# One ring of small feed-forward buffers split into two: thirteen slots for evicted products, three for weight differences

## The chip, the cores and the metric

The kernel runs on one core of one Trainium2 chip. The metric is the device time of one execution in microseconds (us). The engines are TensorE (PE; its weight loads are listed apart as PEld), VectorE (DVE), ScalarE (ACT), GpSimd (POOL) and SyncE (SP), which here issues the transfers.

## The reference

One decoder layer in float32 for 1024 tokens of width 1024: a feed-forward with half weight, a token mixer (dilated window attention beside a gated DeltaNet, merged by gates), a second feed-forward, and a final norm. The change touches the two feed-forwards alone.

```python
def swiglu(x, w_gate, w_up, w_down):
    return (jax.nn.silu(x @ w_gate) * (x @ w_up)) @ w_down

# D_MODEL = 1024, SEQ = 1024, D_FF = 2816
x = x + 0.5 * swiglu(rmsnorm(x, ffn1_norm), ffn1_w_gate, ffn1_w_up, ffn1_w_down)
h = rmsnorm(x, mix_norm)
x = x + hybrid_mixer(h, ...)
x = x + 0.5 * swiglu(rmsnorm(x, ffn2_norm), ffn2_w_gate, ffn2_w_up, ffn2_w_down)
return rmsnorm(x, final_norm)
```

## The kernel before

Every float32 product is made of three products of halves: each operand is split into a high part (a cast, fH for weights) and the remainder (a subtraction, fL), and high x high, low x high and high x low are summed in PSUM. Weights are split by `ff_split`: ACT casts (L207), DVE subtracts (L208). Both results live in rings of nine tiles, fH and fL.

**The hidden part** (`ff_hidden`, once for each feed-forward, at about 46 to 464 us and 2079 to 2515 us) computes silu(x Wg) * (x Wu), one block of 128 hidden columns after another, 22 blocks in all. The first two blocks are done plainly. The other twenty go in ten pairs through `ff_pair` and `ff_products`: a pair of blocks, two halves of the width and two halves of the tokens make a 2x2 matrix product, done with seven products of blocks instead of eight, as in Strassen's scheme. The price is sums and differences of blocks: of the tokens once, of the weights for every pair. The first pair has the order FIRST, the nine others the order STEPS: products 1, 6, 5, 7, 2, 4, 3, each first for the gate matrix (i = 0), then for the up matrix (i = 1). One product of one matrix is 12 matmuls (four pieces of the width by three halves) on 512 tokens, so a pair is 168 matmuls on line L366. They accumulate in four PSUM banks named mm, tC, tM and tA (two tiles each, one for gate and one for up); product 1 is in mm, products 6, 7 and 4 in tC, and product 2 is in mm again.

The weights of a pair come in two transfers of 1 MB (L216, `fraw`, a ring of two: gate and up). `prepare(n, i)` makes the left operand of product n for matrix i out of the four quarters a11, a12, a21, a22 of such a tile. For product 6 DVE makes three differences or sums: s3 = a11 - a21 into a small tile (L323), a21 += a22 (L324), a11 = a21 - a11 (L325); then a11 is split. s3 is the operand of product 7, a21 that of product 5.

After each product the bank is evicted into small tiles of 128 x 512 which `ff_e` gives out: p1 by ACT (L370), u2 (L373) and u3 (L378, L379) by DVE, then silu on ACT (L381, L388, L395, L402) and the product of gate and up on DVE (L383, L390, L397, L404). L378 evicts product 7 and reads bank tC, on which product 4 then accumulates. `ff_store` splits a finished tile (L231 on ACT into `eh`, L232 on DVE) and stores both halves to DRAM (L233, L234, tiles hdH and hdL).

All small tiles come from one ring named "e" with 16 slots: the s3 differences, the evicted products, the halves to store, and, in the down part, the tiles of hidden values. Tiles of one ring get their slots in the order in which the program asks for them, and a tile gets its slot when the tile that held it is done. `weights(...)` of a pair is called before its `products(...)`, so the s3 tiles of a pair stand behind all small tiles of the pair before. Within these limits a scheduler orders each engine's instructions when the program is built, by program order as the priority and by what is ready; each engine then executes its row in order.

**The down part** (`ff_down`) multiplies the hidden values by Wd in chunks of 2, 4, 4, 4, 4, 4 blocks. For a chunk of n blocks it loads 4 x n tiles `hid` (`hid_tile`, L453: a high and a low half of 128 KB each, for block f and token group p of 256 tokens), and for both halves of the output columns and all eight groups of 128 tokens does 3n matmuls (L476) and an eviction (L481, L483). The last tiles of the hidden part are stored while the first tiles of the down part are loaded; the first chunk's tiles of token groups 0 and 1 are asked for by `pre()` before the last pair's products.

Of the kernel before, what the change touches and what calls it, by code (L numbers as in the profile page):

```python
# [8 lines left out]
F32 = mybir.dt.float32  # L9
F32R = mybir.dt.float32r  # L10
# [5 lines left out]
P = 128  # L16
# [53 lines left out]
def psum(C, tag):  # L70
    return C.pp.tile([P, 512], F32, name=tag, tag=tag, bufs=BANKS[tag])
# [60 lines left out]
def cols(w, c0, n=P):  # L132
    return w[:, c0:c0 + n].rearrange("(k p) n -> p k n", p=P)
# [28 lines left out]
def row(C, pool, name, tag, bufs):  # L162
    if pool is C.fx:
        tag, bufs = "big", 12
    return pool.tile([P, D], F32, name=name, tag=tag, bufs=bufs)
# [33 lines left out]
def ff_split(C, src, n=512):  # L199

    nc = C.nc
    H = C.wp.tile([P, 512], F32R, name="fH", tag="fH", bufs=9)
    L = C.wp.tile([P, 512], F32R, name="fL", tag="fL", bufs=9)
    h, l = H[:, :n], L[:, :n]
    if len(src.shape) == 3:
        h, l = [v.rearrange("p (k n) -> p k n", n=src.shape[2]) for v in (h, l)]
    nc.scalar.copy(h, src)  # L207
    nc.vector.tensor_tensor(out=l, in0=src, in1=h.bitcast(F32), op=ALU.subtract)  # L208
    return H, L


def ff_raw(C, src, b):

    raw = C.wp.tile([P, 2048], F32, name="fraw", tag="fraw", bufs=2)
    v = raw[:, :src.shape[1] * b].rearrange("p (a b) -> p a b", b=b)
    C.nc.sync.dma_start(v, src)  # L216
    return v
# [8 lines left out]
def ff_store(C, hid, f, a):  # L226

    nc = C.nc
    s = slice(a * 512, a * 512 + 512)
    H = ff_e(C, "eh", F32R)  # L230
    nc.scalar.copy(H, hid)  # L231
    nc.vector.tensor_tensor(out=hid, in0=hid, in1=H.bitcast(F32), op=ALU.subtract)  # L232
    nc.sync.dma_start(C.hdH[f][:, s], H.bitcast(F32))  # L233
    nc.sync.dma_start(C.hdL[f][:, s], hid)  # L234


def ff_e(C, name="e", dt=F32):
    return C.fx.tile([P, 512], dt, name=name, tag="e", bufs=16)


def ff_plain(C, W, a, n=512, f0=0):

    nc = C.nc
    acc = [(psum(C, "mm"), psum(C, "tC")) for _ in W]
    for n0 in range(0, 512, n):
        for wpair, pair in zip(W, acc):
            for halves, ps in zip(wpair, pair):
                c = slice(a * 512 + n0, a * 512 + n0 + n)
                for k in range(KT):
                    H, L = [v[:, k % 4 * P:k % 4 * P + P] for v in halves[k // 4]]  # L250
                    for i, (x, w) in enumerate(((C.hH, H), (C.hL, H), (C.hH, L))):
                        nc.tensor.matmul(ps[:, n0:n0 + n], w, x[:, k, c], start=k == 0 and i == 0, stop=k == KT - 1 and i == 2)
    for j, (pg, pu) in enumerate(acc):
        sg = ff_e(C)
        nc.scalar.activation(sg, pg, AF.Silu)
        nc.vector.tensor_tensor(out=sg, in0=sg, in1=pu, op=ALU.mult)
        ff_store(C, sg, f0 + j, a)


def ff_blocks(C):  # L260
# [14 lines left out]
    def sums(ks):  # L275
        for k in ks:
            r = []
            for kk, ts in ((k, lo), (k, hi), (4 + k, lo), (4 + k, hi)):
                v = ff_e(C)
                nc.vector.tensor_tensor(out=v, in0=hH[:, kk, ts].bitcast(F32), in1=hL[:, kk, ts].bitcast(F32), op=ALU.add)  # L280
                r.append(v)
            r11, r12, r21, r22 = r
            nc.vector.tensor_tensor(out=r11, in0=r12, in1=r11, op=ALU.subtract)
            split_to(C, *T1[k], r11)
            nc.vector.tensor_tensor(out=r12, in0=r22, in1=r12, op=ALU.subtract)
            split_to(C, *T3[k], r12)
            nc.vector.tensor_tensor(out=r22, in0=r22, in1=r11, op=ALU.subtract)
            split_to(C, *T2[k], r22)
            nc.vector.tensor_tensor(out=r21, in0=r21, in1=r22, op=ALU.subtract)
            keep.append(r21)  # L290
# [14 lines left out]
def ff_pair(C, wg, wu, f0, steps):  # L305


    nc = C.nc
    tt = nc.vector.tensor_tensor
    A = []  # L310
    for w in (wg, wu):
        raw = ff_raw(C, cols(w, f0 * P, 256), 256)
        A.append([raw[:, q * 4:q * 4 + 4, m * P:m * P + P] for m in (0, 1) for q in (0, 1)])
    left = [{}, {}]
    s3 = [None, None]

    def prepare(n, i):
        a11, a12, a21, a22 = A[i]
        if n == 1:
            left[i][1] = ff_split(C, a11)  # L320
        elif n == 6:
            s3[i] = ff_e(C, "s3").rearrange("p (k n) -> p k n", n=P)
            tt(out=s3[i], in0=a11, in1=a21, op=ALU.subtract)  # L323
            tt(out=a21, in0=a21, in1=a22, op=ALU.add)  # L324
            tt(out=a11, in0=a21, in1=a11, op=ALU.subtract)  # L325
            left[i][6] = ff_split(C, a11)
        elif n == 5:
            left[i][5] = ff_split(C, a21)
        elif n == 7:
            left[i][7] = ff_split(C, s3[i])  # L330
        elif n == 2:
            left[i][2] = ff_split(C, a12)
        elif n == 4:
            left[i][4] = ff_split(C, a22)
        else:
            tt(out=a12, in0=a12, in1=a11, op=ALU.subtract)
            left[i][3] = ff_split(C, a12)

    def weights(ns):
        for n in ns:  # L340
            for i in (0, 1):
                prepare(n, i)

    return weights, ff_products(C, f0, left, steps)
# [65 lines left out]
def ff_hidden(C, wg, wu, n0, first=None):  # L410
# [3 lines left out]
    def pre():  # L414
        for p in range(2):
            for f in range(n0):
                held[f, p] = hid_tile(C, f, p)
# [28 lines left out]
    return held  # L446


def hid_tile(C, f, p):

    v = ff_e(C, "hid", F32R).rearrange("p (i t) -> p i t", i=2)
    for i, src in enumerate((C.hdH, C.hdL)):
        C.nc.sync.dma_start(v[:, i].bitcast(F32), src[f][:, p * 256:p * 256 + 256])  # L453
    return v


def ff_down(C, x_dram, wd, chunks, done, pre):

    nc = C.nc
    acc = [None] * NT  # L460
    f0 = 0

    def hid_tiles(p, n):
        return [pre.pop((f0 + k, p)) if (f0 + k, p) in pre else hid_tile(C, f0 + k, p) for k in range(n)]

    def wtiles(nh, n):
        raw = ff_raw(C, wd[f0 * P:(f0 + n) * P, nh * 512:nh * 512 + 512].rearrange("(k p) n -> p k n", p=P), 512)
        return [ff_split(C, raw[:, k]) for k in range(n)]

    def one(ci, t, nh, W, hid):  # L470
        n = len(W)
        ps = psum(C, "tC" if t % 2 else "mm")
        m = slice(t % 2 * P, t % 2 * P + P)
        seq = [(x, k, w) for k in range(n) for x, w in ((0, 0), (0, 1), (1, 0))]
        for i, (x, k, w) in enumerate(seq):
            nc.tensor.matmul(ps, hid[k][:, x, m], W[k][w], start=i == 0, stop=i == len(seq) - 1)  # L476
        if acc[t] is None:
            acc[t] = row(C, C.fx, "acc", None, None)
        a = acc[t][:, nh * 512:nh * 512 + 512]
        if ci == 0:  # L480
            nc.scalar.mul(a, ps, 0.5)  # L481
        else:
            nc.vector.scalar_tensor_tensor(a, ps, 0.5, a, op0=ALU.mult, op1=ALU.add)  # L483

    for ci, n in enumerate(chunks):
        if ci < len(chunks) - 1:
            hid = None
            for nh in (0, 1):
                W = wtiles(nh, n)
                if hid is None:  # L490
                    hid = [hid_tiles(p, n) for p in range(4)]
                for t in range(NT):
                    one(ci, t, nh, W, hid[t // 2])
        else:
            Ws = [wtiles(0, n), wtiles(1, n)]
            hid = [hid_tiles(p, n) for p in range(4)]
            for t in range(NT):
                for nh in (0, 1):
                    one(ci, t, nh, Ws[nh], hid[t // 2])
                done(t, acc[t])  # L500
        if ci == 1:
            for t in range(NT):
                xt = row(C, C.fx, "xt", None, None)
                nc.sync.dma_start(xt, x_dram[t * P:t * P + P])
                nc.vector.tensor_tensor(out=acc[t], in0=acc[t], in1=xt, op=ALU.add)
        f0 += n
# [804 lines left out]
```

## Time and profile before

| | |
|---|---|
| three runs | 2766.78, 2768.46, 2775.07 us; median 2768.46 |
| the profiled execution | 2770.82 us, of which the span of its instructions is 2769.1 |
| mean granted TensorE clock | 0.976 |
| instructions | 35288, of which 13003 matmuls |
| transfers | 300.97 MB, mean 109 GB/s |

The span is that of the profiled execution, which is one run of its own beside the three. In the profile a row of the timeline has the start, the duration, the engine, the line and operation with output and inputs (buffer numbers left out), the shape, and in brackets how long the engine had been idle and what released it. A row of the waits has who waited for whom, the total, the times and the longest, in us. Shapes are written as on the engine, so a 128 x 4 x 128 operand reads 128x512 there. A matmul's duration is longer than its distance to the next, since matmuls overlap.

### The profile page before, as it was taken

Reading aid. Unit: us, or ns where it says so; the run is one execution under the profiler, and the core shown is the slowest. Engines: PE = TensorE matmul, PEld = TensorE weight load, DVE = VectorE, ACT = ScalarE, POOL = GpSimd, SP = SyncE. Lnnn points to the kernel's source line nnn. Section 1 sums busy time; section 2 is a strip of 40 time slices with the busy share of each in tenths; the row PEclk is TensorE's granted clock in tenths of the full one; section 3 lists DMA queues with packets and bytes.
Section 4 is the critical chain, followed back from the end, with each engine's and each line's share of the span. In section 5 each row is a group of like instructions: output and inputs, shape, how many; then the busy total and the mean of one; then the engine's idle time right before and its main releaser. Section 6 shows DMA issues by size and latency. Waiting matters only on the chain. (4 is left out here: it accounts for less than half of the span.)

```text
span 2769.1 us, 35288 instructions
## 1 busy us (share of the span) xinstructions
PE 2638.0 (95%) x13003; PEld 2150.2 (78%) x13003; DVE 1671.3 (60%) x3681; ACT 923.5 (33%) x1644; POOL 307.5 (11%) x175
## 2 busy tenths in 40 slices
PE   7999999999899999899999999899989999999998
PEld 6877877888778777677777777788867787778886
DVE  8866665434342435888777875645657766663535
ACT  5433334112332324432333323144434333333112
POOL 1000000001332131221121211100110000000002
PEclk9999999999999999999998988999999999999999
DMA  4323335552333232321111211345532333336633
GB/s 153 107 94 119 114 107 189 184 174 101 99 79 90 60 105 68 94 62 57 51 43 52 67 45 46 86 156 170 169 125 84 114 118 111 107 109 211 203 117 107
DMA packets 290156, 300.97 MB, mean 109 GB/s; under 512 B 44128, under 2 KB 228672, under 8 KB 289984
## 3 DMA queue, kind: packets, MB, share of 16 engines
q1 hardware_dynamic: 289984, 298.71, 33.7%
q8 instruction: 103, 1.69, 0.3%
q14 instruction: 69, 0.57, 0.1%
HBM read 212.56 MB, written 79.79 MB: 106 GB/s over the span
## 5 line engine op out<-in xcount | busy, mean ns | idle before, releaser
L146 PE MATMUL mm<-hH,wH 128*128 128x512 f32 x1024 | 418.3, 409 | 1.0 <-ACT xp L771 1.0
L146 PE MATMUL mm<-hL,wH 128*128 128x512 f32 x1024 | 419.2, 409 | 0.0
L146 PE MATMUL mm<-hH,wL 128*128 128x512 f32 x1024 | 417.6, 408 | 0.0
L207 ACT CAST fH<-fraw 128x512 fp32r<-128x512 f32 x344 | 203.0, 620 | 530.9 <-PE tC L476 304.7
L208 DVE TENSOR_TENSOR fL<-fraw,fH 128x512 fp32r<-128x512 f32 x344 | 231.9, 702 | 72.0 <-ACT fH L207 69.2
L476 PE MATMUL mm<-fH,hid 128*128 128x512 f32 x704 | 232.8, 390 | 1.8 <-DMA hid<-hdH 1.5
L476 PE MATMUL tC<-fH,hid 128*128 128x512 f32 x704 | 232.2, 389 | 0.0
L146 PEld LDWEIGHTS mm<-hH,wH 128*128 128x128 f32 x1024 | 197.7, 193 | 37.5 <-ACT xp L771 1.4
L146 PEld LDWEIGHTS mm<-hH,wL 128*128 128x128 f32 x1024 | 198.0, 193 | 36.8 <-issue 0.6
L146 PEld LDWEIGHTS mm<-hL,wH 128*128 128x128 f32 x1024 | 198.1, 193 | 36.4 <-issue 0.9
L122 POOL TENSOR_TENSOR wL<-wraw,wH 128x1024 fp32r<-128x1024 f32 (+2 forms) x67 | 161.4, 2412 | 547.7 <-ACT wH L121 442.3
L121 ACT CAST wH<-wraw 128x1024 fp32r<-128x1024 f32 (+2 forms) x101 | 105.0, 1042 | 203.5 <-PE mm L146 149.1
L476 PEld LDWEIGHTS mm<-fH,hid 128*128 128x128 f32 x704 | 132.0, 188 | 31.1 <-DMA hid<-hdH 2.9
L476 PEld LDWEIGHTS tC<-fH,hid 128*128 128x128 f32 x704 | 132.2, 188 | 27.4
L476 PE MATMUL mm<-fL,hid 128*128 128x512 f32 x352 | 137.0, 389 | 0.0
L476 PE MATMUL tC<-fL,hid 128*128 128x512 f32 x352 | 137.0, 389 | 0.0
L366 PE MATMUL mm<-hH,fH 128*128 128x512 f32 x320 | 124.5, 389 | 0.0
L366 PE MATMUL mm<-hL,fH 128*128 128x512 f32 x320 | 124.5, 389 | 0.0
L366 PE MATMUL mm<-hH,fL 128*128 128x512 f32 x320 | 124.5, 389 | 0.0
L483 DVE SCALAR_TENSOR_TENSOR acc<-mm,acc 128x512 f32<-128x512 f32 x80 | 55.3, 691 | 111.2 <-PE mm L476 111.2
L231 ACT CAST eh<-e 128x512 fp32r<-128x512 f32 x88 | 54.7, 622 | 183.9 <-DVE e L397 54.9
L483 DVE SCALAR_TENSOR_TENSOR acc<-tC,acc 128x512 f32<-128x512 f32 x80 | 55.1, 689 | 88.6 <-PE tC L476 88.6
(346 smaller groups left out, 5579.0 us busy)
## 6 DMA issues: line engine op xcount, KB each, us to landing
wraw<-in_w_in_dram SPq DMA_DIRECT2D x64, 512.0 KB, 3.8
fraw<-in_ffn_w_gate_dram SPq DMA_DIRECT2D x22, 1024.0 KB, 5.2
fraw<-in_ffn_w_up_dram SPq DMA_DIRECT2D x22, 1024.0 KB, 7.2
hdH<-eh SPq DMA_DIRECT2D x88, 256.0 KB, 2.0
hdL<-e SPq DMA_DIRECT2D x88, 256.0 KB, 2.0
hid<-hdH SPq DMA_DIRECT2D x176, 128.0 KB, 2.8
hid<-hdL SPq DMA_DIRECT2D x176, 128.0 KB, 2.9
fraw<-in_ffn_w_down_dram SPq DMA_DIRECT2D x20, 1024.0 KB, 5.3
```

Of the source, the lines that this page charges most:

```text
L121: nc.scalar.copy(H[:, :width], raw[:, :width])
L122: (nc.gpsimd if C.pool_split else nc.vector).tensor_tensor(out=L[:, :width], in0=raw[:, :width], in1=H[:, :width].bitcast(F32), op=ALU.sub ...
L146: nc.tensor.matmul(ps[:, n0:n0 + n], w[:, k, :], x[:, k, c0:c0 + n], start=k == 0 and i == 0, stop=k == kt - 1 and i == 2)
L207: nc.scalar.copy(h, src)
L208: nc.vector.tensor_tensor(out=l, in0=src, in1=h.bitcast(F32), op=ALU.subtract)
L231: nc.scalar.copy(H, hid)
L366: nc.tensor.matmul(ps, w, x, start=opens and k == 0 and q == 0, stop=k == 3 and q == 2, skip_group_check=True)
L476: nc.tensor.matmul(ps, hid[k][:, x, m], W[k][w], start=i == 0, stop=i == len(seq) - 1)
L483: nc.vector.scalar_tensor_tensor(a, ps, 0.5, a, op0=ALU.mult, op1=ALU.add)
```

## The change

`ff_e` takes the name of a ring. The ring "e" has 13 slots, a new ring "s3" has 3; together they take the same space. The s3 differences are given out of the new ring. In the down part, the `hid` tiles of the last token group (p = 3), save that of a chunk's first block, come out of it too.

```diff
-def ff_e(C, name="e", dt=F32):
-    return C.fx.tile([P, 512], dt, name=name, tag="e", bufs=16)
+def ff_e(C, name="e", dt=F32, tag="e"):
+    return C.fx.tile([P, 512], dt, name=name, tag=tag, bufs=13 if tag == "e" else 3)
...
-            s3[i] = ff_e(C, "s3").rearrange("p (k n) -> p k n", n=P)
+            s3[i] = ff_e(C, "s3", tag="s3").rearrange("p (k n) -> p k n", n=P)
...
-def hid_tile(C, f, p):
+def hid_tile(C, f, p, tag="e"):
-    v = ff_e(C, "hid", F32R).rearrange("p (i t) -> p i t", i=2)
+    v = ff_e(C, "hid", F32R, tag).rearrange("p (i t) -> p i t", i=2)
...
-        return [pre.pop((f0 + k, p)) if (f0 + k, p) in pre else hid_tile(C, f0 + k, p) for k in range(n)]
+        return [pre.pop((f0 + k, p)) if (f0 + k, p) in pre else hid_tile(C, f0 + k, p, "s3" if p == 3 and k else "e") for k in range(n)]
```

The number of instructions of each engine stays the same, and the rows of TensorE keep their order of products. What moves is shown at three places.

DVE, from one pair of the order STEPS to the next, before the change. Tiles 1792 and 1794 are the next pair's gate and up weights, 1804 and 1812 its s3 tiles; L404 is the last product of the pair that ends.

```order
L404 TENSOR_TENSOR e_1614<-e_1614,e_1629 128x512
L323 TENSOR_TENSOR s3_1804<-fraw_1792 128x512
L323 TENSOR_TENSOR s3_1812<-fraw_1794 128x512
L232 TENSOR_TENSOR e_1614<-e_1614,eh_1787 128x512
L324 TENSOR_TENSOR fraw_1792<-fraw_1792 128x4x128
L324 TENSOR_TENSOR fraw_1794<-fraw_1794 128x4x128
L325 TENSOR_TENSOR fraw_1792<-fraw_1792 128x4x128
L325 TENSOR_TENSOR fraw_1794<-fraw_1794 128x4x128
L208 TENSOR_TENSOR fL_1809<-fraw_1792,fH_1808 128x512
L208 TENSOR_TENSOR fL_1817<-fraw_1794,fH_1816 128x512
```

DVE after the change: the same weight tiles, about the middle of the pair before. The two L208 at the head are that pair's own last splits (product 3), and L378 and L379 evict its product 7.

```order
L208 TENSOR_TENSOR fL_1563<-fraw_1501,fH_1562 128x512
L208 TENSOR_TENSOR fL_1568<-fraw_1503,fH_1567 128x512
L323 TENSOR_TENSOR s3_1804<-fraw_1792 128x512
L208 TENSOR_TENSOR fL_1797<-fraw_1792,fH_1796 128x512
L324 TENSOR_TENSOR fraw_1792<-fraw_1792 128x4x128
L378 TENSOR_TENSOR e_1669<-tC_1601,e_1584 128x512
L325 TENSOR_TENSOR fraw_1792<-fraw_1792 128x4x128
L379 TENSOR_TENSOR e_1669<-tM_1631,e_1669 128x512
L208 TENSOR_TENSOR fL_1801<-fraw_1794,fH_1800 128x512
L323 TENSOR_TENSOR s3_1812<-fraw_1794 128x512
L378 TENSOR_TENSOR e_1685<-tC_1616,e_1599 128x512
L208 TENSOR_TENSOR fL_1809<-fraw_1792,fH_1808 128x512
```

The differences of the next pair moved from behind L404 to between the last splits of a pair and the evictions of its product 7. ACT's casts moved with them: the cast of product 6's gate operand (fH_1808) stood behind the next pair's first eviction (L370), and it now stands behind the silu of this pair's product 7 (L381). Here is ACT before:

```order
L231 CAST eh_1787<-e_1614 128x512
L370 COPY e_1875<-mm_1862 128x512
L207 CAST fH_1808<-fraw_1792 128x512
L370 COPY e_1890<-mm_1877 128x512
L207 CAST fH_1816<-fraw_1794 128x512
```

And here is ACT after, with the same casts fH_1808 and fH_1816:

```order
L207 CAST fH_1796<-fraw_1792 128x512
L207 CAST fH_1800<-fraw_1794 128x512
L381 ACTIVATE e_1669<-e_1669 128x512
L207 CAST fH_1808<-fraw_1792 128x512
L231 CAST eh_1689<-e_1669 128x512
L388 ACTIVATE e_1706<-mm_1571 128x512
L207 CAST fH_1816<-fraw_1794 128x512
```

The casts of product 6 are now issued within the pair before, between its products 7 and 2.

SP at the end of the first hidden part, before the change: the last stores (L233, L234), and then the loads of hid.

```order
L233 DMA hdH19_92<-eh_3435 128x512
L234 DMA hdL19_114<-e_3415 128x512
L233 DMA hdH18_91<-eh_3467 128x512
L234 DMA hdL18_113<-e_3452 128x512
L233 DMA hdH19_92<-eh_3500 128x512
L234 DMA hdL19_114<-e_3330 128x512
L453 DMA hid_3608<-hdH0_73 128x256
```

SP after the change, from the same place:

```order
L453 DMA hid_3862<-hdH1_74 128x256
L453 DMA hid_3862<-hdL1_96 128x256
L233 DMA hdH19_92<-eh_3435 128x512
L234 DMA hdL19_114<-e_3415 128x512
L233 DMA hdH18_91<-eh_3467 128x512
L234 DMA hdL18_113<-e_3452 128x512
L453 DMA hid_4068<-hdH3_76 128x256
L453 DMA hid_4068<-hdL3_98 128x256
L233 DMA hdH19_92<-eh_3500 128x512
L234 DMA hdL19_114<-e_3330 128x512
```

The tile of the second block's last token group (hid_3862) moved from the end of the first chunk's loads to a place ahead of these stores, and two tiles of the second chunk (hid_4068 of block 3, and one of block 4) to places among them.

## The prediction

> **What bounds the kernel now.** I read the page's busy times first, then the wide windows, then TensorE's waits, and last the timeline where these waits lie.
>
> ```profile
> PE 2638.0 (95%) x13003; PEld 2150.2 (78%) x13003; DVE 1671.3 (60%) x3681; ACT 923.5 (33%) x1644; POOL 307.5 (11%) x175
> ...
> 250.00:300.00 50.00, 49.54 (x218) 40.39 (x217) 32.09 (x51) 17.30 (x30) 0.00 (x0) 1.00 0.32 115
> 550.00:600.00 50.00, 50.00 (x222) 41.40 (x222) 20.62 (x31) 7.48 (x12) 0.00 (x0) 1.00 0.45 139
> 1500.00:1550.00 50.00, 48.98 (x295) 40.37 (x292) 31.61 (x101) 12.09 (x24) 8.59 (x5) 0.83 0.13 36
> ...
> PE tC L366 <- ACT fH L207: 8.4, 18, 0.7
> PE mm L476 <- DMA hid<-hdH: 1.5, 2, 1.4
> ```
>
> TensorE is the bound at 95%. In the windows the columns after the length are PE, PEld, DVE, ACT and POOL busy with counts, then the granted clock, the DMA share and GB/s. The first window lies in the hidden part of a feed-forward: it has 218 matmuls where the down part, in the second, has 222, so about four matmuls' time in 50 us is missing, although the clock is 1.00 in both. The third, in the mixer, runs at clock 0.83; the change touches nothing there. The waits (total, times, longest) name what is missing: in the paired products (L366) TensorE waits 18 times for a cast of weights (ACT fH L207), and 18 is the number of pairs with the order STEPS, nine in each feed-forward. One wait a pair, then, before the first matmul of product 6, which opens bank tC.
>
> ```profile
> 195.61 0.39 PE L366 MATMUL mm<-hH,fL 128*128 128x512 f32 x1
> 196.46 0.50 PE L366 MATMUL tC<-t2H,fH 128*128 128x512 f32 x1 [0.46 <-ACT fH L207]
> 196.79 0.40 PE L366 MATMUL tC<-t2L,fH 128*128 128x512 f32 x1
> 197.18 0.50 PE L366 MATMUL tC<-t2H,fL 128*128 128x512 f32 x1
> 197.52 0.39 PE L366 MATMUL tC<-t2H,fH 128*128 128x512 f32 x1
> ...
> 202.28 0.39 PE L366 MATMUL tM<-t1H,fH 128*128 128x512 f32 x1
> ...
> 118.22 0.50 PE L366 MATMUL tC<-t2H,fH 128*128 128x512 f32 x1 [0.41 <-ACT fH L207]
> ...
> 431.06 0.50 PE L366 MATMUL tC<-t2H,fH 128*128 128x512 f32 x1 [0.46 <-ACT fH L207]
> ...
> 2168.98 0.50 PE L366 MATMUL tC<-t2H,fH 128*128 128x512 f32 x1 [0.41 <-ACT fH L207]
> ...
> 2482.09 0.50 PE L366 MATMUL tC<-t2H,fH 128*128 128x512 f32 x1 [0.46 <-ACT fH L207]
> ```
>
> The first column is the start. The named wait is 0.46 us, but the loss is larger: a matmul lasts longer (0.39) than the distance to the next, so starts have to be compared. From 197.52 to the start of product 5 at 202.28 stand 21 matmuls (product 6 has 24, of which three are before): 4.76/21 = 0.2267 us each. The four starts from 195.61 to 197.52 are 0.85, 0.33, 0.39 and 0.34 us apart, 1.91 in all where 4 x 0.2267 = 0.91 would do: 1.00 us is lost in one pair.
>
> The same from the other side. The last four rows are the first product 6 under STEPS and the ninth, in each feed-forward. The period is (431.06 - 118.22)/8 = 39.105 us and (2482.09 - 2168.98)/8 = 39.139. A pair has 7 products x 2 matrices x 12 = 168 matmuls, 168 x 0.2267 = 38.08 us. Lost: 1.03 and 1.06 us a pair, which leaves nothing to look for elsewhere in the pair.
>
> Why product 6's weights come late:
>
> ```profile
> 191.39 0.69 DVE L404 TENSOR_TENSOR e<-e 128x512 f32<-128x512 f32 x1
> 192.00 1.28 DVE L323 TENSOR_TENSOR s<-fraw 128x512 f32<-128x512 f32 x2
> ...
> 193.81 1.28 DVE L324 TENSOR_TENSOR fraw<-fraw 128x512 f32<-128x512 f32 x2
> 195.01 1.28 DVE L325 TENSOR_TENSOR fraw<-fraw 128x512 f32<-128x512 f32 x2
> 196.44 0.69 DVE L208 TENSOR_TENSOR fL<-fraw,fH 128x512 fp32r<-128x512 f32 x1
> ...
> 195.79 0.62 ACT L207 CAST fH<-fraw 128x512 fp32r<-128x512 f32 x1 [1.88 <-DVE fraw L325]
> ```
>
> DVE does the last product of the previous pair (L404), then the six differences, and only then can ACT cast. The s3 tile and the evicted products share one ring, whose slots are handed out in program order, so L323 can't stand ahead of the last eviction.
>
> **The change part by part.** It adds and removes no instruction on any engine; it moves DVE, ACT and SP work of the two feed-forwards.
>
> (1) The six differences and both casts of product 6 move from behind L404 to the middle of the pair before. There the weights have landed, as these rows of the next half pair show:
>
> ```profile
> 205.38 0.38 SPq L216 DMA_DIRECT2D fraw<-in_ffn_w_gate_dram  x1
> 206.58 0.38 SPq L216 DMA_DIRECT2D fraw<-in_ffn_w_up_dram  x1
> ...
> 213.52 0.62 ACT L207 CAST fH<-fraw 128x512 fp32r<-128x512 f32 x1 [0.23 <-DMA fraw<-in_ffn_w_up_dram]
> ...
> 210.64 0.69 DVE L378 TENSOR_TENSOR e<-tC,e 128x512 f32<-128x512 f32 x1 [4.08 <-PE tC L366]
> 213.36 0.69 DVE L378 TENSOR_TENSOR e<-tC,e 128x512 f32<-128x512 f32 x1 [0.73 <-PE tC L366]
> ...
> 218.60 0.39 PE L366 MATMUL tC<-hH,fH 128*128 128x512 f32 x1
> ...
> 221.32 0.39 PE L366 MATMUL tC<-hH,fH 128*128 128x512 f32 x1
> ...
> fraw<-in_ffn_w_gate_dram SPq DMA_DIRECT2D x22, 1024.0 KB, 5.2
> fraw<-in_ffn_w_up_dram SPq DMA_DIRECT2D x22, 1024.0 KB, 7.2
> ...
> ACT fH L207 <- DMA fraw<-in_ffn_w_up_dram: 4.4, 6, 1.3
> ```
>
> The up load, issued at 206.58, lets the cast at 213.52 go, 6.9 us later (median 7.2). After it remain two casts (0.62 each) and about six DVE operations (0.6 to 0.7 each, spread over evictions): product 6's operands should be there by about 220, and its first matmul comes at 196.46 + 39.1 = 235.6 or a microsecond before. The one thing that could still hold the casts is the ring of nine fH and nine fL tiles: a pair takes 14 of each, so product 6's take the slots of tiles that product 7 of the pair before reads, and that product ends at 213.16, when product 2's matmul on mm follows. I therefore take the whole 1.03 and 1.06 us as gone: 9 x 1.03 + 9 x 1.06 = -18.8 us. Bounds: 0 if another operand is late by as much, -18.8 if none is; there is no more in it, since the rest of the pair goes at its pitch. I take the gain's end, because the work moves by some 15 us and the gap is 1.
>
> (2) What now stands behind the loads. DVE runs in order: the first difference waits for the gate load, and behind it queues the gate's eviction of product 7 (L378); the up cast's remainder (L208) waits for the up load, and behind it queues the other L378. Who waits for these: product 4 accumulates into the same banks tC, at 218.60 and 221.32, so the evictions must begin by 218.60 - 0.69 = 217.9 and 220.6. Before, they ran at 210.64 and 213.36. After, the up eviction comes behind the cast (213.52 + 0.62), L208 and L323 (0.69 each): about 215.5, 5.1 us ahead of its limit. The gate's stands behind L323, L208 and L324 of gate weights landed at about 205.38 + 5.2 = 210.6: 0.62 for the cast and three DVE operations, about 213, 4.9 us ahead. Cost 0; the cover is these 5 us, and case D below prices their end.
>
> (3) The ring of 13 instead of 16: eleven evicted tiles a pair fit, and the slot that a new one takes was stored a pair before. Cost 0, bounds 0 to the wait of nearest kind, below in B.
>
> (4) The hid tiles. The tile for the second block's last token group now has a slot of its own, and its two loads go out ahead of the last stores instead of at the end of a burst.
>
> ```profile
> 473.40 0.39 PE L476 MATMUL mm<-fH,hid 128*128 128x512 f32 x1
> 473.98 0.50 PE L476 MATMUL mm<-fH,hid 128*128 128x512 f32 x1 [0.19 <-DMA hid<-hdH]
> ...
> 2523.52 0.19 PEld L476 LDWEIGHTS mm<-fH,hid 128*128 128x128 f32 x1 [1.80 <-DMA hid<-hdH]
> ```
>
> At the first down part the gap is 473.98 - 473.40 - 0.227 = 0.35 us, of a later tile in the burst, which is now two loads shorter (SP takes 0.43 to issue each). The 1.4 us wait that stands in TensorE's list is at the second down part, on the tile whose stores come last; two loads less ahead of it may or may not help. From 0 to 0.35 + 1.4 = 1.75 gain; slower isn't excluded by more than the 0.43 of one issue, as two later tiles' loads (blocks 3 and 4) now go out among the stores. I take -0.4, since the small gap is the one surely behind fewer loads.
>
> (5) The pairs' first stage (order FIRST) has the same work moved into idle time of DVE: 0, with 0.5 either way.
>
> The sum is -18.8 - 0.4 = -19.2 us. The profiled execution took 2770.82 us, 2.36 above the median 2768.46 of the three runs; so 2751.6 for such an execution and 2749.3 for the median.
>
> What the mixer makes of an earlier start is the free term:
>
> ```profile
> 715.00:720.00 5.00, 0.80 (x8) 0.56 (x6) 3.50 (x15) 2.18 (x5) 1.69 (x1) 0.84 0.65 188
> 720.00:725.00 5.00, 3.76 (x16) 3.46 (x17) 1.41 (x3) 3.25 (x5) 3.53 (x2) 0.50 0.08 12
> ```
>
> After an almost idle 5 us the granted clock is 0.50 for the next 5. Where such stretches fall can shift with a mixer that starts some 9.5 us earlier; the runs' own spread, 2766.78 to 2775.07, is what I allow for it. In the pairs the clock is 1.00 (250 to 300) with the gaps in, so closing them buys time once, and no clock. The Trainium skill (TensorE: Matmul & The Clock Gate, Part 1) says that the gate halves the clock only after an idle window of about 3.4 us; the rows agree, the idle stretch at 715 paying with 0.50 and gaps of about 1 us paying nothing.
>
> **The rivals.**
>
> A. The gap closes and nothing takes its place: 2749.3.
>
> B. Another operand of product 6 is late, or a slot of the smaller ring. The nearest wait is the second of the same gap, the weight load for fL:
>
> ```profile
> 197.18 0.19 PEld L366 LDWEIGHTS tC<-t2H,fL 128*128 128x128 f32 x1 [0.43 <-DVE fL L208]
> ```
>
> About half a microsecond a pair stays, 18 x 0.5 = 9: 2758. Against it: the remainder fL is written right behind the cast, some 15 us ahead too.
>
> C. The gap stays, 2768.5: the total of slots is 16 as before, so if a lack of slots made it, nothing changes. Against it: L323 waits in the rows for its place behind L404, not for a store, and the new order of DVE has it half a pair earlier. The Trainium skill (Perfetto Trace Analysis, Identifying Performance Opportunities, Optimization Strategy) reads a gap that repeats on the engine to be saturated as a possible lack of buffers, their count or size; by the count nothing would be gained here, and the trace speaks for the place in the ring.
>
> D. Slower: DVE stands waiting for the up load with the up eviction of product 7 behind it. It has to begin by 220.6; cast, L208 and L323 take 2.0, so it decides when the load lands more than 220.6 - 2.0 - 206.58 = 12.0 us after its issue, and the gain is eaten at about 13.1. At twice the median, 14.4 us, each of 18 pairs loses 2.4: 2749.3 + 43 = 2792. Against it: no wait for that load in this stretch (150 to 450 us) was over 1.3 us, and the DMA share there is 0.32.
>
> **How the numbers follow.** A 0.81, B 0.08, C 0.06, D 0.05. A alone lies between 2744 (the larger hid gain and a run 4 lower) and 2756 (a run as far above its median as 2775.07 is). Within 0.3%, about what a measurement here can tell from no change, is 2760.2 to 2776.8. The range 2742 to 2762 holds A and B and leaves out C and D, 0.11. Faster: A and most of B, 0.87; same: C and the rest of B, 0.08; slower: D, 0.05.
>
> **What would show it.** Right: the list of waits has no ACT fH L207 ahead of tC L366 under STEPS; product 6's first matmul starts 0.23 us after product 1's last; the period is 38.1 us; 222 matmuls stand in 250 to 300; L323 runs around 211 to 215, and L378 about 2 us later than before with no wait of PE tC or PE mm behind it. Wrong: a period near 38.6 (B), 39.1 (C), or over 40 with PE waiting for DVE e L378 (D); or a mixer longer by more than 6 us at an unchanged sum of the feed-forwards.

## The result and the profile after

Twenty runs of each kernel, in turns: before 2773.20 us median, after 2754.61. One run of the kernel before took 4317.94 us and is not in the ratio. The ratio of the mean times of the others is 0.9944, with a 95% interval from 0.9928 to 0.9959: faster, by 15.5 us, with an interval from 11 to 20. The kernel's mean granted clock differs from run to run, and most of the width of that interval goes with it, as shown further down.

The page's busy times and the window from 250 to 300 us of the changed kernel, with the same columns as before:

```profile
PE 2628.5 (96%) x13003; PEld 2154.7 (78%) x13003; DVE 1668.0 (61%) x3681; ACT 931.7 (34%) x1644; POOL 307.2 (11%) x175
...
250.00:300.00 50.00, 50.00 (x222) 41.40 (x221) 36.14 (x58) 19.55 (x35) 0.00 (x0) 1.00 0.29 106
```

The hidden part now has 222 matmuls in 50 us, as many as the down part had, with no idle time at all. The timeline of TensorE at the same place of the pair, and the first product 6 of the first and the ninth pair under STEPS in each feed-forward:

```profile
194.26 0.39 PE L366 MATMUL mm<-hH,fL 128*128 128x512 f32 x1
194.49 0.39 PE L366 MATMUL tC<-t2H,fH 128*128 128x512 f32 x1
...
118.33 0.39 PE L366 MATMUL tC<-t2H,fH 128*128 128x512 f32 x1
...
422.97 0.39 PE L366 MATMUL tC<-t2H,fH 128*128 128x512 f32 x1
...
2155.06 0.39 PE L366 MATMUL tC<-t2H,fH 128*128 128x512 f32 x1
...
2459.70 0.39 PE L366 MATMUL tC<-t2H,fH 128*128 128x512 f32 x1
```

Product 6 begins 0.23 us after product 1's last matmul. The period is (422.97 - 118.33)/8 = 38.08 us, and 38.08 in the second feed-forward, the 168 x 0.2267 of a pair without a gap. What TensorE waits for in the pairs and the down parts is now this (total, times, longest); the 18 waits for a cast are gone, and two waits in the pairs' first stage are new:

```profile
PE tC L366 <- ACT t2H L152: 1.4, 2, 0.8
...
PE mm L476 <- DMA hid<-hdH: 0.4, 1, 0.4
...
PE mm L476 <- DMA hid<-hdL: 0.3, 1, 0.3
```

Where the time went, by the starts of the first and last matmul of each part in the two profiles:

| part | before | after | difference |
|---|---|---|---|
| pairs, first feed-forward | 390.16 | 381.94 | -8.22 |
| down, first | 249.00 | 248.79 | -0.21 |
| mixer | 1411.68 | 1406.29 | -5.39 |
| pairs, second feed-forward | 390.35 | 381.65 | -8.70 |
| down, second | 240.98 | 240.08 | -0.90 |
| ahead of the first pair, and behind the last matmul | 86.93 | 87.15 | +0.22 |
| span | 2769.1 | 2745.9 | -23.2 |

The pairs won 16.9 us, and all parts but the mixer 17.8. The 5.4 us in the mixer are not put down to the change: TensorE's instructions there stand in the same order in both kernels (those of DVE and ACT too, save six for the second feed-forward's weights at its end), and other profiles of the same rows differ by more, as shown further down.

### The profile page after: what moved, and what is told of

The parts are those of the page before. It is cut to its first block, busy times and chain, and to the rows that moved or that the text cites. A ratio compares the mean times of both kernels' runs of the same rounds, so it can differ in the third digit from the quotient of the medians.

```text
span 2745.9 us, 35416 instructions
## 1 busy us (share of the span) xinstructions
PE 2628.5 (96%) x13003; PEld 2154.7 (78%) x13003; DVE 1668.0 (61%) x3681; ACT 931.7 (34%) x1644; POOL 307.2 (11%) x175
## 5 line engine op out<-in xcount | busy, mean ns | idle before, releaser
L207 ACT CAST fH<-fraw 128x512 fp32r<-128x512 f32 x344 | 210.6, 621 | 599.8 <-PE tC L476 304.7
L208 DVE TENSOR_TENSOR fL<-fraw,fH 128x512 fp32r<-128x512 f32 x344 | 239.1, 701 | 114.5 <-ACT fH L207 113.0
```

## The experiments

The first four kernels here ran once each, beside one run of the kernel before (2763.03 us): 2774.59, 2769.61, 2757.21 and 2875.93 us, in the order of this section. Runs of one kernel spread over as much as 23 us, so the first three are read by the stretches of their profiles. The last three ran six to eight times, in turns with 14 runs of the kernel before.

**Only the hid tiles in the ring of three**, the s3 differences back among the thirteen:

```diff
-            s3[i] = ff_e(C, "s3", tag="s3").rearrange("p (k n) -> p k n", n=P)
+            s3[i] = ff_e(C, "s3").rearrange("p (k n) -> p k n", n=P)
```

> Only the hid tiles of the last token group use the ring of three; the s3 differences are back in the ring of 13. My theory (the gap of a pair goes because the s3 differences no longer stand behind the last eviction in one ring): the period of a pair is 39.1 us as before, the wait of TensorE for the cast ahead of product 6 is there 18 times, the paired stretches are 390.2 and 390.4 us; the down parts keep what they won, 0.2 and 0.9 us. Rival (the hid tiles, or the smaller ring, make the gain): the period falls to 38.1, the paired stretches to about 382.

From its list of waits and TensorE's timeline, the first and ninth pair of the first feed-forward:

```profile
PE tC L366 <- ACT fH L207: 8.2, 18, 0.5
...
118.20 0.50 PE L366 MATMUL tC<-t2H,fH 128*128 128x512 f32 x1 [0.40 <-ACT fH L207]
...
431.06 0.50 PE L366 MATMUL tC<-t2H,fH 128*128 128x512 f32 x1 [0.46 <-ACT fH L207]
```

The period is 39.11 us, the paired stretches 390.20 and 390.13, the down parts 248.92 and 240.15. The gap is all there: neither the hid tiles nor the smaller ring closes it.

**One ring of 17 slots** in the kernel before.

```diff
-    return C.fx.tile([P, 512], dt, name=name, tag="e", bufs=16)
+    return C.fx.tile([P, 512], dt, name=name, tag="e", bufs=17)
```

> The kernel before with one ring of 17 slots instead of 16, which is all that the memory holds. Rival (a lack of slots makes the gap): the gap of 1.03 us gets smaller, the period falls below 39.1, by at least 0.1. My theory (the place in the ring, not the number of slots): period 39.1 us, paired stretches 390.2 and 390.4 us, the wait for the cast 18 times, nothing changed beyond 0.3 us a stretch.

The same two views:

```profile
PE tC L366 <- ACT fH L207: 8.2, 18, 0.5
...
118.13 0.51 PE L366 MATMUL tC<-t2H,fH 128*128 128x512 f32 x1 [0.40 <-ACT fH L207]
...
430.99 0.50 PE L366 MATMUL tC<-t2H,fH 128*128 128x512 f32 x1 [0.46 <-ACT fH L207]
```

Period 39.11, paired stretches 390.20 and 390.14. One slot more buys nothing: it isn't one missing slot that makes the gap. The Trainium skill (Perfetto Trace Analysis, Identifying Performance Opportunities, Optimization Strategy) lists the buffer count and the tile sizes as what a repeated gap can come from; this gap came from neither, as 17 slots were no better than 16, and it went with 13 + 3 slots of the same size.

**Only the s3 differences in the ring of three**, all hid tiles among the thirteen:

```diff
-... hid_tile(C, f0 + k, p, "s3" if p == 3 and k else "e") for k in range(n)]
+... hid_tile(C, f0 + k, p, "e") for k in range(n)]
```

> Only the s3 differences use the ring of three; all hid tiles are in the ring of 13, which is less than the 16 tiles of a chunk. My theory: the period of a pair is 38.08 us, the paired stretches about 382 us, as in the changed kernel; the down parts pay for the 13 slots, since tiles of the last token group wait for those of the first: 0 to 5 us for each of ten chunks. Rival (the hid tiles make the gain): period 39.1.

The first and ninth product 6 of the first feed-forward, and the waits of TensorE in the down part:

```profile
118.57 0.39 PE L366 MATMUL tC<-t2H,fH 128*128 128x512 f32 x1
...
423.21 0.39 PE L366 MATMUL tC<-t2H,fH 128*128 128x512 f32 x1
...
PE mm L476 <- DMA hid<-hdL: 2.1, 5, 1.0
...
PE mm L476 <- DMA hid<-hdH: 1.2, 2, 1.0
```

Period 38.08 in both feed-forwards, paired stretches 381.95 and 381.40: the whole gain of the pairs comes from the s3 differences. The down parts take 253.66 and 243.47, which is 4.7 and 2.5 us more than before, about 0.7 for each of the ten chunks of four blocks, at the low end of what was expected. A chunk wants 16 hid tiles, so the part of the change that lets three of them use the other ring is what keeps the smaller ring from costing 7 us.

**The s3 tiles asked for early, in one ring of 16.** The write of s3 (L323; L340 in this code) stands in the program ahead of the products of the pair before:

```diff
...
         if f0 == NF - 2:
             pre()
+        else:
+            nxt = ff_pair(C, wg, wu, f0 + 2, STEPS)
+            nxt[0](())
         products(B, STEPS)
```

`nxt[0](())` writes the two s3 tiles of the next pair.

> One ring of 16 as before, no second ring; the code asks for and writes the next pair's s3 tiles ahead of this pair's products. This puts L323 of the up weights, which waits for their load, ahead of the eviction of product 6 (L373) on DVE, and product 7 can't begin before that eviction. Theory of the place: the gap ahead of product 6 goes with one ring too (no wait for the cast under STEPS save the first pair's). Case D of the prediction (evictions queue behind a load): the up load goes out about 9.5 us after a pair's product 6 begins and lands 5.4 later, L323 and L373 take 1.4, so product 7 starts at about 16.3 instead of 10.9: 5.4 us lost in each of 16 pairs, period about 43.5, about 85 us slower than the changed kernel. Rival (the load lands in time, or other work hides it): period 38.1 to 39.1.

Its timeline in one pair (SP, DVE, ACT, TensorE), TensorE's waits, and a window of 6.8 us in that pair with the columns as before:

```profile
221.05 0.38 SPq L216 DMA_DIRECT2D fraw<-in_ffn_w_up_dram  x1
...
223.51 0.69 DVE L340 TENSOR_TENSOR s<-fraw 128x512 f32<-128x512 f32 x1 [2.50 <-DMA fraw<-in_ffn_w_gate_dram]
223.59 0.62 ACT L207 CAST fH<-fraw 128x512 fp32r<-128x512 f32 x1 [3.30 <-DMA fraw<-in_ffn_w_gate_dram]
224.12 1.06 ACT L371 COPY e<-mm 128x512 f32<-128x512 f32 x2
...
226.27 0.69 DVE L340 TENSOR_TENSOR s<-fraw 128x512 f32<-128x512 f32 x1
226.88 1.28 DVE L374 TENSOR_TENSOR e<-tC,e 128x512 f32<-128x512 f32 x2
...
224.75 0.50 PE L367 MATMUL mm<-hH,fH 128*128 128x512 f32 x1 [2.21 <-ACT e L371]
227.62 0.80 PE L367 MATMUL tC<-t3H,fH 128*128 128x512 f32 x1 [2.37 <-DVE e L374]
...
PE tC L367 <- DVE e L374: 39.6, 16, 3.3
PE mm L367 <- ACT e L371: 38.9, 16, 3.5
...
225.20:232.00 6.80, 4.43 (x11) 3.49 (x11) 3.51 (x6) 0.00 (x0) 0.00 (x0) 0.50 0.07 25
```

The wait ahead of product 6 goes here too, in one ring. But both evictions of product 6 (L374) stand behind the two s3 writes, the first of which waits for the gate load (2.50 us here), and product 7 waits for them, 16 times. A second wait was not expected: the two copies of product 1 (L371), which ask for their slots behind the s3 tiles, stand on ACT behind the cast of the next pair's gate weights and so wait for the gate load as well, and the first matmul of product 2 on bank mm, which stands ahead of product 7, waits for them, 16 times. The paired stretches are 441.9 and 443.2 us, the periods 44.7 to 48.2 instead of the expected 43.5, and the single run took 2875.9 us. The waits are not all of it. Behind these gaps the granted clock is 0.50, as the window shows, where it was 1.00 in the pairs of the kernel before and the changed one. In this pair the two gaps cost 5.0 us by the starts of matmuls (222.15, 224.75, 227.62), and some ten matmuls behind them are about 0.43 us apart instead of 0.2267, which is about 2 us more. The direction of the wait has turned round: instead of s3 behind the evictions, the evictions are behind s3. That is the mechanism of case D at another place, product 6's evictions behind the gate load instead of product 7's behind the up load, and with the clock it costs about 7.6 us a pair against the 38.08.

**One ring of 16, the s3 tiles asked for between products 7 and 2** of the pair before:

```diff
...
-        products(B, STEPS)
+        products(B, STEPS[:4])
+        if f0 < NF - 2:
+            nxt = ff_pair(C, wg, wu, f0 + 2, STEPS)
+            nxt[0](())
+        products(B, STEPS[4:])
```

> One ring of 16, no second ring, hid tiles as in the kernel before; the code writes the next pair's s3 tiles between this pair's products 7 and 2, so that they stand behind the evictions of products 1, 6 and 7 in the ring and ahead of the others. The first pair under STEPS isn't moved. My theory (place in the ring): eight of nine gaps of each feed-forward close without a second ring: period 38.08, the first distance stays 28.1, paired stretches 381.9 each, down parts as before (249.0 and 240.9); ratio 0.9925 to 0.9955. Rival (a ring of their own is needed): period 39.1, ratio 1.0. Case D: L323 of the up weights stands behind both evictions of product 7 (L378) on DVE, so that no eviction waits for the load, and none of the loss of s3_early_one_ring is seen.

```profile
118.57 0.50 PE L367 MATMUL tC<-t2H,fH 128*128 128x512 f32 x1 [0.40 <-ACT fH L207]
...
423.64 0.39 PE L367 MATMUL tC<-t2H,fH 128*128 128x512 f32 x1
...
PE tC L367 <- ACT fH L207: 0.8, 2, 0.4
```

The next pair's loads are asked for at this place too; they go out 6.96 us after product 6 begins, as in the changed kernel. One wait in each feed-forward is left, at the first pair under STEPS, which this code doesn't move; the other sixteen are gone, and later periods are 38.08. (The first period is 38.51, since 0.4 us of the first gap lie behind the first matmul.) Paired stretches 382.10 and 382.02, ratio 0.9936 (0.9911 to 0.9961). A second ring isn't needed for the gain. What decides is where in the order of one ring the s3 tiles stand: behind the evictions that are due soon, ahead of those that are not.

**The first pair's s3 tiles in the ring of thirteen.** In the changed kernel two waits were new, in the stage under FIRST:

> The changed kernel, but the s3 tiles of the first pair (order FIRST) come out of the ring of 13; the nine other pairs keep the ring of three. In the changed kernel one matmul of product 6 in FIRST, which waits for the last token sum t2H, stands five matmuls earlier on TensorE, and 1.35 and 1.06 us are lost there (0.25 and 0.18 before). My theory: with the old order of FIRST these come back. From the first product 6 of FIRST to that of the first pair under STEPS 27.2 us each (28.34 and 28.05 in the changed kernel), period 38.08, paired stretches 380.9 and 380.8; the time 2 us below the changed kernel, 0.9925 to 0.995 of the kernel before. Rival (the loss in FIRST comes with the next pair's early work on DVE, not with the order on TensorE): 28.3 and 28.0 stay, stretches 381.9 and 381.7.

```diff
-            s3[i] = ff_e(C, "s3", tag="s3").rearrange("p (k n) -> p k n", n=P)
+            s3[i] = ff_e(C, "s3", tag="e" if steps is FIRST else "s3").rearrange("p (k n) -> p k n", n=P)
```

TensorE's timeline in FIRST, of the kernel before, of the changed kernel, and of this one, with ACT's cast of t2H in the first two (in the changed kernel also of the second feed-forward, with the last sum on DVE ahead of it, L287):

```profile
93.77 0.39 PE L366 MATMUL tC<-t2L,fH 128*128 128x512 f32 x1
94.14 0.50 PE L366 MATMUL tC<-t2H,fH 128*128 128x512 f32 x1
...
93.46 0.63 ACT L152 ACTIVATE t2H<-e 128x512 fp32r<-128x512 f32 x1 [0.57 <-DVE e L287]
```

```profile
92.48 0.39 PE L366 MATMUL tC<-t2H,fL 128*128 128x512 f32 x1
93.72 0.73 PE L366 MATMUL tC<-t2H,fH 128*128 128x512 f32 x2 [0.85 <-ACT t2H L152]
94.29 0.39 PE L366 MATMUL tC<-t2L,fH 128*128 128x512 f32 x1
...
91.90 0.68 DVE L287 TENSOR_TENSOR e<-e 128x512 f32<-128x512 f32 x1
...
92.52 0.62 ACT L207 CAST fH<-fraw 128x512 fp32r<-128x512 f32 x1 [0.47 <-DMA fraw<-in_ffn_w_gate_dram]
93.04 0.62 ACT L152 ACTIVATE t2H<-e 128x512 fp32r<-128x512 f32 x1
...
2129.00 0.68 DVE L287 TENSOR_TENSOR e<-e 128x512 f32<-128x512 f32 x1
...
2129.93 0.62 ACT L207 CAST fH<-fraw 128x512 fp32r<-128x512 f32 x1 [0.79 <-DMA fraw<-in_ffn_w_gate_dram]
2130.45 0.62 ACT L152 ACTIVATE t2H<-e 128x512 fp32r<-128x512 f32 x1
```

```profile
94.26 0.50 PE L366 MATMUL tC<-t2H,fH 128*128 128x512 f32 x1
...
117.78 0.39 PE L366 MATMUL tC<-t2H,fH 128*128 128x512 f32 x1
...
422.42 0.39 PE L366 MATMUL tC<-t2H,fH 128*128 128x512 f32 x1
```

In the changed kernel the matmul that needs the last token sum, t2H, came after 92.48, 1.24 us later than the matmul before it; in the kernel before, other matmuls were put ahead of it and it lost little. From FIRST's first matmul, the 168 matmuls of a pair take 39.22 and 38.93 us in the changed kernel, 38.39 and 38.31 before, and 38.39 and 38.29 here, where 168 distances of 0.2267 are 38.08. So 1.14 and 0.85 us are lost in the changed kernel, 0.31 and 0.23 before, and 0.31 and 0.21 here; the 1.35 and 1.06 of the expectation were too large. The distance from FIRST's product 6 to the next pair's is 27.51 and 27.42 us; the expected 27.2 is 120 distances with nothing lost, and the small loss of the old order stays.

The order on TensorE is not all of it. In the changed kernel the next pair's gate load goes out at 86.58 us, before it at 97.10 and here at 97.22, and in the changed kernel ACT's cast of these weights, which waits for the load, stands ahead of the cast of t2H. In the kernel before, t2H's cast begins 0.72 us after L287, and in all of them the matmul follows 0.68 later. So without the other cast the matmul could have begun at about 93.3 instead of 93.72 (it was due at 92.71), and in the second feed-forward at about 2130.4, just when it was due, instead of 2131.13. By this estimate the early cast makes 0.4 us of the loss in the first feed-forward and nearly all of it in the second; in the old order, with five more matmuls ahead, the same delay would have been covered. This kernel puts both back, so it doesn't tell them apart. Paired stretches 381.11 and 381.01: 0.8 and 0.6 us less than in the changed kernel. By their stretches this is the best of the kernels here; the ratio, 0.9939 (0.9917 to 0.9961), can't tell it from the changed one.

**The changed kernel once more:**

> The changed kernel once more, on the chip of the two others. My theory: the paired stretches repeat to 0.3 us (381.9 and 381.7) and the mixer, whose instructions stand in the same order in every kernel here, differs from the 1406.3 us of the first profile by up to 8 us with the granted clock: the spread of the times comes from there. Rival (the mixer's 5.4 us less than before are an effect of the change): it is again 1405 to 1408 us.

Paired stretches 382.00 and 381.78, which repeat to 0.13 us. The mixer took 1399.9 us, 6.4 less than in the first profile. In the other profiles, the kernel before and the experiments in the order of this section, it took 1411.7, 1416.5, 1410.7, 1408.0, 1413.0, 1408.6 and 1414.0 us, with the same instructions in the same order. The rival (again 1405 to 1408) fell. Both profiles of the changed kernel lie below all others. The mean granted clock fits the second, 0.979, but not the first: 0.976 is the clock of the first profile of the kernel before as well, whose mixer was 5.4 us longer. The cause of these 5.4 us stays open. The ratio of this set was 0.9918 (0.9894 to 0.9942).

The spread of the runs goes with the clock. A straight line through all 55 runs with a clock on record (14 of the kernel before, the 20 of the changed kernel in the result, and all of the last three kernels here), with one slope and a level for each set, falls by 2.30 us for each 0.001 of the mean granted clock, and leaves 2.2 us of scatter where the runs of one set spread over as much as 23. At a clock of 0.975 the levels are:

| kernel | runs | us at clock 0.975 | pairs, both feed-forwards |
|---|---|---|---|
| before | 14 | 2773.1 | 780.5 |
| changed | 20 | 2754.9 | 763.6 |
| changed again | 6 | 2753.2 | 763.8 |
| one ring, s3 between 7 and 2 | 7 | 2756.0 | 764.1 |
| first pair's s3 in e | 8 | 2750.8 | 762.1 |

So the change is worth 18.2 to 19.9 us at an equal clock, of which the 19.9 compares runs of one set on one chip; whether the 20 runs were on that chip is not on record. The order of the kernels is that of their paired stretches. A level is uncertain by 0.5 to 1 us, so the distances among the changed kernels are not read further. The Trainium skill (TensorE: Matmul & The Clock Gate, Part 1) says that a gate halves the clock after an idle window, that the window runs free, and that the number of cold matmuls of one kernel varies from run to run; this agrees with a time that goes with the clock while the paired stretches, at clock 1.00, repeat to 0.13 us. That the windows' phase is what differs was not tried.

## Why the prediction was right, and where not

The forecast was A, 2749.3 us and faster by 19.2; measured were 2754.61 and, by the ratio, 15.5, or 18.6 by the medians of twenty runs. Of the 5.3 us between 2749.3 and 2754.61, 4.7 are the base: the median of three runs, 2768.46, stood that much below that of twenty.

- The gap (-18.8). Right in place and cause, and near in size: with FIRST's loss put back, the pairs won 8.22 + 0.83 = 9.05 and 8.70 + 0.62 = 9.32 us, 18.4 in all, against 9.3 and 9.5 in the sum. The runs with one part alone put it on the s3 differences, and the two variants with one ring show that it is their place in the order of slots.
- FIRST (0, with 0.5 either way). Wrong: it cost 1.14 - 0.31 = 0.83 and 0.85 - 0.23 = 0.62 us, about 1.5 in all. The step looked at DVE alone, which has idle time there. It did not look at TensorE's row, where a matmul with a late operand moved five places ahead, nor at ACT's, where a cast that waits for the next pair's load came in ahead of that operand's cast.
- The evictions behind the loads (cost 0). Right in cost, and the two microseconds of delay that it gave were wrong. SP, DVE and TensorE in the changed kernel's pair:

```profile
201.45 0.38 SPq L216 DMA_DIRECT2D fraw<-in_ffn_w_gate_dram  x1
204.04 0.38 SPq L216 DMA_DIRECT2D fraw<-in_ffn_w_up_dram  x1
...
206.56 0.69 DVE L323 TENSOR_TENSOR s<-fraw 128x512 f32<-128x512 f32 x1 [2.55 <-DMA fraw<-in_ffn_w_gate_dram]
...
208.51 0.68 DVE L378 TENSOR_TENSOR e<-tC,e 128x512 f32<-128x512 f32 x1
...
211.51 0.68 DVE L378 TENSOR_TENSOR e<-tC,e 128x512 f32<-128x512 f32 x1
...
216.25 0.39 PE L366 MATMUL tC<-hH,fH 128*128 128x512 f32 x1
```

DVE does stand waiting for the gate load (2.55 us here). But the load goes out 6.96 us after the pair's product 6 begins, and not 8.92 as before, because the last weights of the pair are split earlier too (which the step had not counted, and which is 2 us of its cover); so the first L378 starts 14.02 us after that point, and before it was 14.18. Product 4's first matmul on tC leaves 216.25 - 0.69 - 208.51 = 7.1 us of cover, where 4.9 was forecast.

- The ring of 13 (0): right. No gap appears in a pair, and hid_only has the period of before with 13 slots.
- The hid tiles (-0.4, from 0 to -1.75). Measured -0.21 and -0.90, in the second profile -0.12 and -0.47; the kernel with 17 slots, with nothing meant for the down part, had +0.51 and -0.49, and the one with s3 between products 7 and 2 had +0.09 and -0.86. A gain of this size isn't shown. What the step had not priced is the loss that this part prevents: 7.2 us in s3_only.
- The mixer: the allowance of the runs' spread held the 5.4 us of the profile, whose cause stays open; they are why one profile against one (-23.2) overstates the change.

B and C fell with the period of 38.08, C's reading (the number of slots) with the ring of 17 besides. D did not come true here, and its mechanism did in the kernel that asks for s3 early.

## What to carry to other kernels

Tiles that share a ring get their slots in the order of the program, so work that could run early is held behind every tile asked for before it, and a seventeenth slot changed nothing in that: look at what the rows do, ring by ring, before adding slots. Move such a tile behind the evictions that are due soon and no further, since a write that waits for a transfer holds up everything behind it on its engine. After a change of rings, compare the rows of the bounding engine everywhere, and the rows that make its operands: a matmul that moved a few places ahead and a cast that moved ahead of its operand's cost 1.5 of the 19 us here. And price a gap of some microseconds with the clock behind it: in the kernel that asks for s3 early it was 0.50 there.

## What was not expected of the hardware

With the same instructions in the same order the mixer took from 1399.9 to 1416.5 us in nine profiles, and the time of a run followed its mean granted clock at 2.30 us for each 0.001, while the paired stretches of one kernel repeat to 0.13 us; so a difference of 2 us between kernels shows in the stretches of a profile long before it shows in the runs.
